# Even and odd columns of a matmul's moving operand in two halves of its tile

## The chip, the cores and the metric

The kernel runs on one core of one Trainium2 chip. The metric is the device time of one execution in microseconds (us); for the kernel before it is 2790.34 us, the median of three runs (2790.34 to 2790.83).

## The reference

One inference step of a decoder trunk with one layer, model width 2048, all in float32. 16 learned meta tokens and 256 prompt tokens form one sequence; 8 further tokens are single decode steps with recurrent states of their own. All 280 tokens share the weights:

```python
def swiglu(x, w_gate, w_up, w_down):
    return (jax.nn.silu(x @ w_gate) * (x @ w_up)) @ w_down
...
x = layer_norm(ALPHA * x + 0.5 * swiglu(x, f1_g, f1_u, f1_d), ln1_g, ln1_b)
m, s_ret, s_hg = token_mixer(x, pos, s_ret, s_hg, prompt, w_in, lb, hg_norm_g, w_out)
x = layer_norm(ALPHA * x + m, ln2_g, ln2_b)
x = layer_norm(ALPHA * x + 0.5 * swiglu(x, f2_g, f2_u, f2_d), ln3_g, ln3_b)
```

The FFN width is 5504. `token_mixer` projects x by one matrix to 10 x 2048 columns (q, k, v and gate of a retention branch with 8 heads, the same of an HGRN2 branch with 16 heads, and two merge gates), runs both recurrences in chunks, merges them and projects by `w_out`. The outputs are the tokens after the third norm (without the meta tokens) and the new states.

## The kernel before

Activations lie transposed: the 128 partitions hold 128 features, the columns are tokens. So x is 16 tiles of 128 x 280 (T = 280), and from the mixer's merge on 128 x 264 (TL = 264, without the meta tokens). Weights are the stationary operand in blocks of 128 x 128, and tokens are the moving operand.

For precision without plain-fp32 matmuls, each operand is split in two tiles of the rounded type fp32r: a high part (ScalarE casts, L198 for activations, L163 for weights) and a low part, the rest (VectorE subtracts, L199 and L164). `dense` (L179, its matmul is L193) then issues three products for each weight block: high x high, high weight x low activation, low weight x high activation. All add into one PSUM bank over the `nk` blocks of a sum.

The stages in order, each a stream of dense products on TensorE:

- FFN 1 up: 43 pairs of gate and up blocks, two pairs to a group of four banks, over 16 feature tiles, 280 columns (trace name `up`). The result goes through SiLU and a product into `sg` and is split into the hidden tiles `hh` and `hl` (43 of each).
- FFN 1 down: 16 output blocks over the 43 hidden tiles, 280 columns (`dn`).
- Mixer: the input projection in 8 units (head pairs); per unit first f, q_h, i_h, q_r, k_r, v_r, then the gates of the unit before (g_r, a_r, g_h, a_h), each two blocks of 128 features over 16 feature tiles (`pj_...`). The parts f, i_h, k_r, v_r have 280 columns, the other six 264: their moving operand starts at token 16. Two coroutines a unit (`mix_hg`, `mix_ret`) do the recurrences with small matmuls; `pump` moves each on after a number of product steps that its `yield` names.
- w_out: 16 blocks over 16 merge tiles `yh`, `yl`, 264 columns (`wo`).
- FFN 2 up and down, as FFN 1 with 264 columns.

The order of instructions on TensorE is written out by hand (it is the program's); a scheduler orders the other engines by priority. Weights are loaded by `stream` (L145) from SyncE's queue in units of 8 blocks, three buffers deep.

`x_tiles` (L231) hands out the moving tiles of x: each has 296 columns (XP), of which 280 or 264 are used from a start column that differs from tile to tile (0, 4, 8 or 12). `Norm` keeps a running residual `d`: `residual` (L262, operations L269 and L270) reads the high and low parts back, `shifted` (L302) may write a "lead" version of x before the mean is known (L318, L319: the rows by the norm's gain, one column of ones behind the tokens, one column of the bias behind that), and `normalise` (L357) writes the final x parts (L364, L365). `first` (L336) runs the first group of the next stage on the lead version.

## Time and profile before

| | |
|---|---|
| median of the runs | 2790.34 us |
| profiled execution's own span | 2787.6 us |
| TensorE busy, granted clock | 2777.1 us, 1.00 |
| TensorE weight loads busy | 2752.6 us |
| VectorE busy | 1735.2 us |
| ScalarE busy | 1362.0 us |
| DMA moved | 536.27 MB, mean 192 GB/s |

The profiled execution is not timed apart from its span: the span runs from the first to the last instruction, and the 2.7 us to the runs' median lie around it. In the profile PE is the matmul side of TensorE and PEld its weight loads, which overlap the matmuls; DVE is VectorE, ACT is ScalarE, POOL is GpSimd and SP is SyncE with the DMA queue. A matmul row's duration reaches from its start to its modelled end and overlaps the next one, so the step from one matmul to the next is shorter than the duration.

### The profile page before, as it was taken

Reading aid. Unit: us, or ns where it says so; the run is one execution under the profiler, and the core shown is the slowest. Engines: PE = TensorE matmul, PEld = TensorE weight load, DVE = VectorE, ACT = ScalarE, POOL = GpSimd, SP = SyncE. Lnnn points to the kernel's source line nnn. Section 1 sums busy time; section 2 is a strip of 40 time slices with the busy share of each in tenths; the row PEclk is TensorE's granted clock in tenths of the full one; section 3 lists DMA queues with packets and bytes.
Section 4 is the critical chain, followed back from the end, with each engine's and each line's share of the span. In section 5 each row is a group of like instructions: output and inputs, shape, how many; then the busy total and the mean of one; then the engine's idle time right before and its main releaser. Section 6 shows DMA issues by size and latency. Waiting matters only on the chain.

```text
span 2787.6 us, 54458 instructions
## 1 busy us (share of the span) xinstructions
PE 2777.1 (100%) x22576; PEld 2752.6 (99%) x22576; DVE 1735.2 (62%) x2937; ACT 1362.0 (49%) x2116; POOL 3.3 (0%) x38
## 2 busy tenths in 40 slices
PE   9999999999999999999999999999999999999999
PEld 9999999999999999999999999999999999999998
DVE  5444444464469777777777777776884444446544
ACT  5433343333356565656565656564554444444333
POOL 0000000000000000000000000000000000000000
PEclk9999999999999999999999999999999999999999
DMA  7555555555556676667666766665555555555554
GB/s 234 168 173 168 173 169 172 171 170 169 172 189 206 223 255 196 231 203 230 203 230 199 235 202 232 201 212 181 181 177 182 182 182 182 181 182 180 181 181 138
DMA packets 154584, 536.27 MB, mean 192 GB/s; under 512 B 17696, under 2 KB 25696, under 8 KB 154336
## 3 DMA queue, kind: packets, MB, share of 16 engines
q1 hardware_dynamic: 154048, 532.50, 59.4%
q8 instruction: 177, 2.90, 0.4%
q14 instruction: 71, 0.58, 0.1%
q10 hardware_dynamic: 288, 0.29, 0.0%
HBM read 502.12 MB, written 30.61 MB: 191 GB/s over the span
## 4 chain that ended last, share of the span: by engine, by line
PE 98%; DVE 1%; ACT 0%; issue 0%; DVEq 0%
PE up L193 37%; PE dn L193 19%; PE pj_f L193 4%; PE pj_v_r L193 4%; PE pj_i_h L193 4%; PE pj_g_r L193 3%; PE pj_q_h L193 3%; PE pj_g_h L193 3%; PE pj_q_r L193 3%; PE pj_a_h L193 3%; PE wo L193 3%; PE pj_a_r L193 3%; PE pj_k_r L193 3%; PE pqr L997 1%; PE psr L966 0%; PE psc L949 0%
## 5 line engine op out<-in xcount | busy, mean ns | idle before, releaser
L164 DVE TENSOR_TENSOR wlo<-raw,whi 128x1024 fp32r<-128x1024 f32 (+1 forms) x869 | 1062.5, 1223 | 866.4 <-ACT whi L163 863.3
L163 ACT CAST whi<-raw 128x1024 fp32r<-128x1024 f32 (+1 forms) x870 | 909.2, 1045 | 1104.2 <-PE up L193 478.5
L193 PE MATMUL up<-xl,whi 128*128 128x280 f32 (+1 forms) x2688 | 765.4, 288 | 0.0
L193 PE MATMUL up<-xh,wlo 128*128 128x280 f32 (+1 forms) x2688 | 765.1, 288 | 0.0
L193 PE MATMUL up<-xh,whi 128*128 128x280 f32 (+1 forms) x2688 | 764.3, 287 | 0.0
L193 PEld LDWEIGHTS up<-xh,wlo 128*128 128x128 f32 x2688 | 503.0, 188 | 0.2 <-DVE wlo L164 0.2
L193 PEld LDWEIGHTS up<-xh,whi 128*128 128x128 f32 x2688 | 503.0, 188 | 0.0
L193 PEld LDWEIGHTS up<-xl,whi 128*128 128x128 f32 x2688 | 502.7, 188 | 0.0
L193 PE MATMUL dn<-hh,whi 128*128 128x280 f32 (+1 forms) x1376 | 397.1, 289 | 0.0
L193 PE MATMUL dn<-hl,whi 128*128 128x280 f32 (+1 forms) x1376 | 395.8, 288 | 0.0
L193 PE MATMUL dn<-hh,wlo 128*128 128x280 f32 (+1 forms) x1376 | 395.7, 288 | 0.0
L193 PEld LDWEIGHTS dn<-hl,whi 128*128 128x128 f32 x1376 | 259.0, 188 | 0.1
L193 PEld LDWEIGHTS dn<-hh,whi 128*128 128x128 f32 x1376 | 258.9, 188 | 0.1
L193 PEld LDWEIGHTS dn<-hh,wlo 128*128 128x128 f32 x1376 | 258.7, 188 | 0.0
L193 PE MATMUL pj_g_r<-xh,whi 128*128 128x264 f32 x256 | 79.2, 309 | 0.0
L193 PE MATMUL pj_v_r<-xh,whi 128*128 128x280 f32 x256 | 75.9, 297 | 0.0
L193 PE MATMUL pj_g_h<-xh,whi 128*128 128x264 f32 x256 | 75.2, 294 | 0.0
L193 PE MATMUL pj_k_r<-xh,whi 128*128 128x280 f32 x256 | 75.0, 293 | 0.0
L193 PE MATMUL pj_i_h<-xh,whi 128*128 128x280 f32 x256 | 74.8, 292 | 0.0
L193 PE MATMUL pj_v_r<-xl,whi 128*128 128x280 f32 x256 | 74.6, 292 | 0.0
L193 PE MATMUL pj_i_h<-xl,whi 128*128 128x280 f32 x256 | 74.6, 291 | 0.0
L193 PE MATMUL pj_k_r<-xl,whi 128*128 128x280 f32 x256 | 74.6, 291 | 0.0
(379 smaller groups left out, 5219.4 us busy)
## 6 DMA issues: line engine op xcount, KB each, us to landing
raw<-in_w_up SPq DMA_DIRECT2D x343, 512.0 KB, 3.4
raw<-in_w_in SPq DMA_DIRECT2D x320, 512.0 KB, 3.7
raw<-in_w_dn SPq DMA_DIRECT2D x172, 512.0 KB, 3.4
smr<-in_sr SPq DMA_DIRECT2D x32, 512.0 KB, 4.8
out_srs<-smr SPq DMA_DIRECT2D x32, 512.0 KB, 6.3
raw<-in_w_out SPq DMA_DIRECT2D x32, 512.0 KB, 3.5
smh<-in_sg SPq DMA_DIRECT2D x16, 512.0 KB, 3.6
out_sgs<-smh SPq DMA_DIRECT2D x16, 512.0 KB, 6.2
```

The source lines that it names most:

```text
L163: nc.scalar.copy(hi[:, j:jn, :], raw[:, j:jn, :])
L164: nc.vector.tensor_tensor(out=lo[:, j0:j1, :], in0=raw[:, j0:j1, :], in1=hi[:, j0:j1, :].bitcast(F32), op=ALU.subtract)
L193: nc.tensor.matmul(o, w, t, start=start, stop=stop)
L997: nc.tensor.matmul(pq[32 * j : 32 * j + 32, 256 * e : 256 * e + 256], qdr[:, c, 32 * b : 32 * b + 32], sms[2 * e + c][:, j, :], start=c == ...
```

## The change

Every moving tile of a dense product (x, hidden and merge tiles, both parts) is kept in two halves: the first half holds the even columns, the second the odd ones. `Halves` presents such a tile as a pattern of (pair, even or odd), so that reading it in order gives column 0 from the first half, column 0 of the second half, then the next of each. `dense` reads the moving operand so and writes PSUM as pairs, in the usual column order. What writes these tiles (the splits, the lead, the final norm) and what reads them back (the residual) goes through the same pattern, while the other operand is read as pairs in order. The halves are 148 columns long in the x tiles, 140 or 132 in the hidden tiles and 132 in the merge tiles. The differing start columns of the x tiles are gone. The lead version sets two columns of ones and works on an even number of columns.

```diff
 
 WP = P + 4
 XP = 296
+XH = XP // 2
 
 WARM = 11
 
@@ -51,6 +52,23 @@
 SCORES = ((0, 0, SEQ, P), (SEQ, P - NMETA, 2 * P - P + NMETA, P), (2 * SEQ - P + NMETA, SEQ - NMETA, NMETA, LP - 2 * P))
 NSC = SCORES[2][0] + SCORES[2][2]
 GAMMA = [1.0 - 2.0 ** (-5.0 - h) for h in range(HR)]
+
+
+def pairs(x):
+
+    return x.rearrange("p (b a) -> p b a", a=2)
+
+
+class Halves:
+
+
+    def __init__(self, tile, half, n):
+        self.all = tile.rearrange("p (a b) -> p b a", b=half)
+        self.n = n
+
+    def __getitem__(self, cols):
+        c0, c1, _ = cols.indices(self.n)
+        return self.all[:, c0 // 2 : c1 // 2, :]
 
 
 def ffn_up_groups():
@@ -184,8 +202,8 @@
             todo = []
             for i in range(n):
                 wh, wl = block()
-                h, l = xhi[k][:, cols[i]], xlo[k][:, cols[i]]
-                o = outs[i][:, : h.shape[1]]
+                h, l = xhi[k][cols[i]], xlo[k][cols[i]]
+                o = pairs(outs[i][:, : 2 * h.shape[1]])
                 todo.append([(o, wh, h, k == 0, False), (o, wh, l, False, False), (o, wl, h, False, k == nk - 1)])
 
             for x in zip(*todo) if parts_in_turn else todo:
@@ -195,6 +213,8 @@
                 hook(k)
 
     def split(hi, lo, x):
+        if isinstance(hi, Halves):
+            hi, lo, x = hi[:], lo[:], pairs(x)
         nc.scalar.copy(hi, x)
         nc.vector.tensor_tensor(out=lo, in0=x, in1=hi.bitcast(F32), op=ALU.subtract)
 
@@ -229,9 +249,8 @@
     xl = [None] * KC
 
     def x_tiles(c, which, n=T):
-        for e, (x, nm) in enumerate(((xh, "xh"), (xl, "xl"))):
-            o = 4 * ((2 * c + e) // 8 % 2) + 8 * (c % 2) * e
-            x[c] = xp.tile([P, XP], F32R, tag=f"{nm}{c}", name=f"{nm}{which}_{c}")[:, o : o + n]
+        for x, nm in ((xh, "xh"), (xl, "xl")):
+            x[c] = Halves(xp.tile([P, XP], F32R, tag=f"{nm}{c}", name=f"{nm}{which}_{c}"), XH, n)
 
     def row_tile(name, n=T):
         return rp.tile([P, n], F32, tag=name, name=name)
@@ -263,13 +282,13 @@
 
             n = self.n
             a = ALPHA if self.whole else 2.0 * ALPHA
-            self.dx[m] = dx = row_tile(f"d{m}", T + 1)
+            self.dx[m] = dx = row_tile(f"d{m}", T + 2)
             self.d[m] = d = dx[:, :n]
-            x0 = xh[m].shape[1] - n
-            nc.vector.scalar_tensor_tensor(out=d, in0=xl[m][:, x0:].bitcast(F32), scalar=a, in1=other, op0=ALU.mult, op1=op)
-            nc.vector.scalar_tensor_tensor(out=d, in0=xh[m][:, x0:].bitcast(F32), scalar=a, in1=d, op0=ALU.mult, op1=ALU.add)
+            x0, o = xh[m].n - n, pairs(d)
+            nc.vector.scalar_tensor_tensor(out=o, in0=xl[m][x0:].bitcast(F32), scalar=a, in1=pairs(other), op0=ALU.mult, op1=op)
+            nc.vector.scalar_tensor_tensor(out=o, in0=xh[m][x0:].bitcast(F32), scalar=a, in1=o, op0=ALU.mult, op1=ALU.add)
             if self.lead:
-                nc.gpsimd.memset(dx[:, n : n + 1], 1.0)
+                nc.gpsimd.memset(dx[:, n : n + 2], 1.0)
 
         def chunk(self, m, f):
             if self.d[m] is not None:
@@ -314,12 +333,12 @@
             if self.lead:
                 x_tiles(m, f"g{self.which}", n + 2)
                 g = self.g[:, m : m + 1]
-                dx = self.dx[m][:, : n + 1]
-                nc.scalar.activation(xh[m][:, : n + 1], dx, AF.Identity, scale=g)
+                dx = pairs(self.dx[m][:, : n + 2])
+                nc.scalar.activation(xh[m][:], dx, AF.Identity, scale=g)
                 nc.vector.scalar_tensor_tensor(
-                    out=xl[m][:, : n + 1], in0=dx, scalar=g, in1=xh[m][:, : n + 1].bitcast(F32), op0=ALU.mult, op1=ALU.subtract)
-                nc.vector.tensor_copy(xh[m][:, n + 1 : n + 2], self.bs[:, 0, m : m + 1])
-                nc.vector.tensor_copy(xl[m][:, n + 1 : n + 2], self.bs[:, 1, m : m + 1])
+                    out=xl[m][:], in0=dx, scalar=g, in1=xh[m][:].bitcast(F32), op0=ALU.mult, op1=ALU.subtract)
+                nc.vector.tensor_copy(xh[m][n:][:, 0, 1:], self.bs[:, 0, m : m + 1])
+                nc.vector.tensor_copy(xl[m][n:][:, 0, 1:], self.bs[:, 1, m : m + 1])
 
         def stats(self):
             n = self.n
@@ -361,9 +380,9 @@
                 sub(d, d, self.mean)
                 nc.vector.scalar_tensor_tensor(out=d, in0=d, scalar=g, in1=self.r, op0=ALU.mult, op1=ALU.mult)
                 x_tiles(c, self.which, self.n)
-                nc.scalar.activation(xh[c], d, AF.Identity, bias=b)
+                nc.scalar.activation(xh[c][:], pairs(d), AF.Identity, bias=b)
                 nc.vector.scalar_tensor_tensor(
-                    out=xl[c], in0=d, scalar=b, in1=xh[c].bitcast(F32), op0=ALU.add, op1=ALU.subtract)
+                    out=xl[c][:], in0=pairs(d), scalar=b, in1=xh[c][:].bitcast(F32), op0=ALU.add, op1=ALU.subtract)
 
         def finish(self, out):
 
@@ -426,8 +445,8 @@
                     sg = hp.tile([P, n], F32, tag="sg", name=f"sg{m}", bufs=2)
                     nc.scalar.activation(sg, outs[j][:, :n], AF.Silu)
                     mul(sg, sg, outs[ng + j][:, :n])
-                    hh[m] = hp.tile([P, n], F32R, tag=f"hh{m}", name=f"hh{m}")
-                    hl[m] = hp.tile([P, n], F32R, tag=f"hl{m}", name=f"hl{m}")
+                    hh[m] = Halves(hp.tile([P, n], F32R, tag=f"hh{m}", name=f"hh{m}"), n // 2, n)
+                    hl[m] = Halves(hp.tile([P, n], F32R, tag=f"hl{m}", name=f"hl{m}"), n // 2, n)
                     split(hh[m], hl[m], sg)
             if before is not None:
 
@@ -490,7 +509,7 @@
         def parts(pool, cs):
             for n, x in (("yh", yh), ("yl", yl)):
                 for c in cs:
-                    x[c] = pool.tile([P, TL], F32R, tag=f"{n}{c}", name=f"{n}{c}")
+                    x[c] = Halves(pool.tile([P, TL], F32R, tag=f"{n}{c}", name=f"{n}{c}"), TL // 2, TL)
 
         yh, yl, ys = [None] * KC, [None] * KC, [None] * KC
         parts(yp, range(EARLY))
```

## Prediction, on record before the result

> **What bounds the kernel now.** I read the page first: busy times, the granted clock and the chain that ended last.

> ```profile
> span 2787.6 us, 54458 instructions
> ...
> PE 2777.1 (100%) x22576; PEld 2752.6 (99%) x22576; DVE 1735.2 (62%) x2937; ACT 1362.0 (49%) x2116; POOL 3.3 (0%) x38
> ...
> PEclk9999999999999999999999999999999999999999
> ...
> PE 98%; DVE 1%; ACT 0%; issue 0%; DVEq 0%
> ```

> TensorE is busy for 2777.1 of 2787.6 us, 98% of the last chain is its own, and the granted clock is full in all forty slices. So nothing that the other engines do is worth more than a few microseconds, and the time is a number of products times what one product takes. The chain in order of time tells what one takes (start, length, what, how many):

> ```profile
> 5.57 532.05 PE up L193 x4128
> ...
> 557.39 246.59 PE dn L193 x1914
> ...
> 1950.98 67.56 PE wo L193 x555
> ...
> 2027.90 491.27 PE up L193 x4056
> 2537.92 233.51 PE dn L193 x1914
> ```

> In FFN 1 the moving tiles have 280 columns, and a product takes 532.05/4128 = 128.9 ns and 246.59/1914 = 128.8 ns. With 264 columns it is 67.56/555 = 121.7, 491.27/4056 = 121.1 and 233.51/1914 = 122.0 ns. These are the two numbers that the change can move.

> The next question is whether they are as low as the engine goes. The groups by shape, and one tile's own row (lowest/median/highest ns), answer that. A row's duration is longer than the step from one product to the next, since products overlap (291 ns for a step of 128.9), but differences between widths are differences of the step:

> ```profile
> L193 PE MATMUL up<-xh,whi 128*128 128x280 f32 x1376 | 393.1, 291 | 0.0
> ...
> L193 PE MATMUL up<-xh,whi 128*128 128x264 f32 x1312 | 371.2, 283 | 0.0
> ...
> L966 PE MATMUL psr<-vs,ks 128*128 128x256 f32 x112 | 15.8, 281 | 0.0
> ...
> L729 PE MATMUL pl<-Qm,K 128*128 128x192 f32 x64 | 11.7, 326 | 0.0
> ...
> L1011 PE MATMUL por<-dtab,vtr 128*128 128x256 f32 x32 | 9.5, 379 | 0.0
> ...
> L1011 PE MATMUL por<-dtab,vtr 128*128 128x144 f32 x32 | 6.5, 286 | 0.0
> ```

> ```profile
> L204 PE MATMUL pd<-prodsmh,ones_r x8: 393/396/399, 865.1 to 1785.3; 128*128 128x512 f32 x8
> ```

> Lines 193, 966 and 204 multiply the rounded type fp32r in one pass; lines 1011 and 729 multiply plain fp32, which the trace records as two passes. One fp32 pass costs (379 - 286)/112 = 0.830 ns a column. One fp32r product costs (396 - 281)/256 = 0.449 ns a column. Twice the speed of an fp32 pass would be 0.415, so the fp32r stream runs 0.034 ns a column (8%) behind. This loss grows with the columns (the rows of 256 and 512 give it), so it is not one fixed price for each new weight block; it belongs to the moving stream, the thing that the change re-lays. The fp32 row at 192 columns, whose moving operand is three separate runs of 64, lies on the fp32 line: 286 + 48 x 0.830 = 326. So a second dimension in the moving pattern, and two jumps in it, cost nothing at the fp32 pace.

> **The change part by part.** It adds and removes no matmul, no weight load, no DMA and no wait. It changes the address of each column: consecutive columns come from places 592 bytes apart (x tiles, half of 296 columns), 560 or 528 bytes apart (hidden tiles, half of 280 or 264) or 528 (merge tiles), and back by that minus 4. PSUM is still written in order.

> *Products.* Of the loops, 280 columns go through 43 x 2 x 16 x 3 = 4128 products of FFN 1 up, 16 x 43 x 3 = 2064 of FFN 1 down, and 64 x 16 x 3 = 3072 of the input projection (f, i_h, k_r, v_r): 9264. At 264 columns there are 4128 and 2064 of FFN 2, 96 x 16 x 3 = 4608 of the projection and 16 x 16 x 3 = 768 of w_out: 11568. (The first groups of two stages have two columns more, which I leave out.) No row shows a moving tile read at alternating places, so the price has two ends. If two open places let the stream run at its full pace, a product of 280 loses 280 x 0.034 = 9.5 ns and one of 264 loses 9.0: 9264 x 9.5 + 11568 x 9.0 = 88 + 104 = 192 us less. If each column has to be fetched by itself and the stream falls to the pace of an fp32 pass, it is 0.830 - 0.449 = 0.381 ns a column more, 106.7 and 100.6 ns a product: 988 + 1164 = 2152 us more. The nearest rows do not decide: the three-run row tells of two jumps in 192 columns at half the pace, here there is a jump at every column at full pace. I take the gain, because a loss that grows with the columns at full pace and is nil at half pace looks like one place of the store that cannot answer fast enough, and two places used in turn each have to answer at only half the rate.

> [...]

> *What is late next if products shorten.* Weight loading comes close. A group of short products with full weight blocks shows its pace:

> ```profile
> 886.90 0.84 PE pl L757 x8
> ```

> That is 105 ns for a product of 64 columns, whose columns alone take 64 x 0.830 = 53 ns, so I read 105 as the load of 128 weights. Shortened products would take 128.9 - 9.5 = 119.4 and 121.4 - 9.0 = 112.4 ns, still above it. The other engines come next (start and end of the stretch, its length, then busy times of PE, PEld, DVE, ACT and POOL with counts, clock, DMA share, GB/s):

> ```profile
> 804.00:866.00 62.00, 61.98 (x483) 61.46 (x482) 58.34 (x123) 43.16 (x75) 0.99 (x2) 1.00 0.60 193
> 866.00:900.00 34.00, 32.72 (x264) 31.95 (x264) 33.05 (x85) 21.47 (x54) 0.00 (x0) 1.00 0.68 226
> ...
> 1180.00:1864.00 684.00, 684.00 (x5741) 671.21 (x5739) 508.69 (x1039) 395.06 (x735) 0.79 (x8) 1.00 0.66 217
> ```

> From 804 to 900 us VectorE is busy 91.4 of 96 us, so that stretch cannot shorten: its 747 products give back 747 x 9.3 ns = 7 us of the gain. In the steady mixer one head pair takes 139.28 us (two starts of the same piece):

> ```profile
> 1319.91 4.63 PE pj_f L193 x36
> ...
> 1459.19 4.63 PE pj_f L193 x36
> ```

> It holds 8 x 48 products of 280 and 12 x 48 of 264, which would save 384 x 9.5 + 576 x 9.0 = 8.8 us, 6%. VectorE's share there goes from 74% to 79%. The mixer's threads wait for a fixed number of product steps, and those steps get shorter while the vector chains do not, so I count a third of it as lost over some 7.5 such periods: 22 us.

> *Writers and readers of the halves.* The splits (L198, L199), the normalise pair (L364, L365), the lead pair (L318, L319) and the two residual operations (L269, L270) keep their counts and sizes (one column more in the lead), but write or read with the jump. Rows:

> ```profile
> L198 ACT CAST hh<-sg x86: 406/418/427, 35.9 to 2520.1; 128x280 fp32r<-128x280 f32 x43, 128x264 fp32r<-128x264 f32 x43
> ```

> ```profile
> L199 DVE TENSOR_TENSOR hl<-sg,hh 128x280 fp32r<-128x280 f32 x43 | 17.3, 444 | 0.0
> ...
> L199 DVE TENSOR_TENSOR prodvbh<-pr,prodsmh 128x256 fp32r<-128x256 f32 x40 | 15.5, 418 | 0.0
> ...
> L207 DVE TENSOR_TENSOR pr<-Q,K 128x256 f32<-128x256 f32 x24 | 9.4, 420 | 0.2
> ...
> L365 DVE SCALAR_TENSOR_TENSOR xl<-d,lnp,xh 128x280 fp32r<-128x280 f32 x16 | 7.4, 499 | 0.0
> ...
> L901 DVE TENSOR_TENSOR vtr<-vtr,cen 128x512 f32<-128x512 f32 x8 | 5.5, 690 | 0.2
> ```

> The lower end is nil: the 24 products "pr" read every second or fourth column and take 420 ns where unbroken operands take 418. The upper end is twice the time a column, (690 - 444)/232 = 1.06 ns, or 0.30 us an operation. I take nil for ScalarE and most of VectorE, whose extra 0.6 us per hidden pair would lie beside some 24.7 us of products (192 x 128.9 ns) in which both engines are about half idle. Only at 804 to 900 us is the cover gone: 16 operations of line 365 at up to 0.30 us, 5 us, which I count. The last hidden tile is used after 41 x 3 products of the down pass (15.9 us), so stage ends stay covered. The wider memset on POOL is not on the chain.

> Sum: 192 - 7 - 22 - 5 = 158 us; I take 150, since the whole of the 0.034 going is the upper end. The median of the runs is 2790.34 us, 2.7 above the profiled span, with only the time around the span between; 2790.3 - 150 = 2640 us.

> **Rivals.** First, on the other side: half pace. The moving port keeps one place open, each column opens a new one, and products take 129 + 107 = 236 and 121.4 + 100.6 = 222 ns. Everything else is then hidden under TensorE, the mixer included: 2790 + 2152 = 4942 us. It decides from the point where a jump costs more than the 0.034 ns a column now lost. [...] Against: the store serves more than one stream at once already, since each product's weights load under the one before. [...] Second, a part of that: only some jumps are slow. With one column in four at the fp32 pace the loss is a quarter, 538 us, and the time 3328 us. Third, the loss is not in the place that is read (a clock crossing, say): products keep 129 and 121 ns, and only VectorE's 5 us at 804 to 900 us may show: 2790 to 2795 us.

> **How the numbers follow.** Gain 0.48; half pace 0.36; a part of it 0.10; no effect 0.06, of which 0.05 within 0.2% (5.6 us, about what a measurement of this kernel can tell from no change) and 0.01 above. So faster 0.48, same 0.05, slower 0.47. The likeliest single case is the gain, with a range of its own of 2598 (all 192 us) to 2740 us (a third of the 150 us). As both signs hold most of the chance, the range has to reach over the half pace: 2595 to 4960 us.

> **What would show it.** Right: the long pieces of the chain at some 120 ns a product in FFN 1 and 113 in FFN 2, the row of 280 columns near 282 ns, DVE's share above 64%, new waits of PE on DVE in the mixer and around 850 us. Half pace: 236 and 222 ns, the row near 398 ns, VectorE's share at 35%. No effect: the rows as they are. The splits' rows (418, 444 ns) tell whether a jump costs the other engines anything. The prediction is wrong in its main step if the products get longer.

## The result

The changed kernel takes 2630.63 us (median of four runs, 2628.61 to 2631.78) against 2790.34 us before: a ratio of 0.9428, 95% interval 0.9414 to 0.9441. That is 160 us less; the prediction was 2640 us. The profiled execution took 2630.44 us with a span of 2628.7 us.

The page of the changed kernel, its busy times, clock, and chain by engine:

```profile
span 2628.7 us, 54448 instructions
...
PE 2602.0 (99%) x22576; PEld 2569.1 (98%) x22576; DVE 1758.9 (67%) x2937; ACT 1388.5 (53%) x2116; POOL 3.3 (0%) x38
...
PE 83%; DVE 9%; DMA 4%; ACT 2%; issue 1%; SPq 0%; DVEq 0%; ACTq 0%
```

TensorE has the same 22576 matmuls in 175 us less, and is no longer the whole chain: VectorE has 9% of it and transfers 4%, where both had next to nothing. The chain in order of time (start, length, what, how many) has the long stages:

```profile
10.66 488.37 PE up L211 x4096
499.04 17.88 PE dn L211 x150
517.38 228.10 PE dn L211 x1914
...
2397.14 215.32 PE dn L211 x1914
```

A product of 280 columns now takes 488.37/4096 = 119.2 and 228.10/1914 = 119.2 ns (128.9 before), one of 264 columns 215.32/1914 = 112.5 ns (122.0). The groups by shape of the changed kernel:

```profile
L211 PE MATMUL up<-xh,whi 128*128 128x280 f32 x1376 | 381.4, 283 | 0.2 <-ACT whi L181 0.2
...
L211 PE MATMUL up<-xh,wlo 128*128 128x264 f32 x1312 | 362.3, 276 | 0.2 <-DVE wlo L182 0.2
...
L985 PE MATMUL psr<-vs,ks 128*128 128x256 f32 x112 | 16.1, 284 | 0.2 <-DVE ks L957 0.2
```

The small products `psr`, which the change leaves in one piece, have not got shorter (281 before, 284 now), so it is the layout and not the clock. What got longer are the operations that write the halves, on VectorE (by shape) and ScalarE (the tile's row):

```profile
L219 DVE TENSOR_TENSOR hl<-sg,hh 128x280 fp32r<-128x280 f32 x43 | 24.8, 655 | 0.2 <-ACT hh L218 0.2
...
L384 DVE SCALAR_TENSOR_TENSOR xl<-d,lnp,xh 128x280 fp32r<-128x280 f32 x16 | 10.0, 711 | 0.1
...
L289 DVE SCALAR_TENSOR_TENSOR d<-xh,d 128x280 f32<-128x280 f32 x16 | 6.7, 450 | 0.1
```

```profile
L218 ACT CAST hh<-sg x86: 674/698/732, 34.9 to 2380.7; 128x280 fp32r<-128x280 f32 x43, 128x264 fp32r<-128x264 f32 x43
```

Writing in turn costs 0.2 to 0.3 us an operation (444 to 655, 499 to 711, 418 to 698 ns). Reading in turn costs next to nothing: line 289, which reads x back, takes 450 ns where it took 440 before:

```profile
L270 DVE SCALAR_TENSOR_TENSOR d<-xh,d 128x280 f32<-128x280 f32 x16 | 7.0, 440 | 0.0
```

By stage, from the starts of the first products of each stage in the two traces (us; head pairs are the mixer's units):

| stage | before | after | change | dense products |
|---|---|---|---|---|
| FFN 1 up | 532.1 | 493.1 | -39.0 | 4128 of 280 |
| FFN 1 down | 266.4 | 246.4 | -19.9 | 2064 of 280 |
| mixer, head pair 1 | 79.5 | 82.3 | +2.8 | 576 |
| mixer, head pair 2 | 154.4 | 156.6 | +2.1 | 960 |
| mixer, the other six | 886.1 | 836.1 | -50.1 | 6144 |
| w_out | 94.5 | 89.7 | -4.8 | 768 of 264 |
| FFN 2 up | 500.6 | 469.7 | -30.9 | 4128 of 264 |
| FFN 2 down | 252.1 | 232.5 | -19.6 | 2064 of 264 |

At 9.7 ns a product of 280 and 9.0 of 264 the six later pairs could give 2304 x 9.7 + 3840 x 9.0 = 57 us and gave 50. The first two could give 14 and took 5 more. Those, 7 us of the later pairs, some 6 of FFN 2 up's 37 and 2 of w_out's 7 are where the gain did not arrive.

### The profile page after: what moved, and what is told of

It is laid out like the page before. It is cut to its first block, busy times and chain, and to the rows that moved or that the text cites. A ratio compares the mean times of both kernels' runs of the same rounds, so it can differ in the third digit from the quotient of the medians.

```text
span 2628.7 us, 54448 instructions
## 1 busy us (share of the span) xinstructions
PE 2602.0 (99%) x22576; PEld 2569.1 (98%) x22576; DVE 1758.9 (67%) x2937; ACT 1388.5 (53%) x2116; POOL 3.3 (0%) x38
## 4 chain that ended last, share of the span: by engine, by line
PE 83%; DVE 9%; DMA 4%; ACT 2%; issue 1%; SPq 0%; DVEq 0%; ACTq 0%
PE up L211 35%; PE dn L211 18%; DVE wlo L182 3%; PE pj_q_h L211 3%; PE pj_v_r L211 3%; PE pj_f L211 3%; PE pj_k_r L211 3%; PE pj_i_h L211 3%; PE pj_q_r L211 2%; PE pj_g_r L211 2%; PE pj_g_h L211 2%; PE pj_a_h L211 2%; PE pj_a_r L211 2%; PE wo L211 2%; DMA smr<-in_sr 1%
## 5 line engine op out<-in xcount | busy, mean ns | idle before, releaser
L211 PE MATMUL up<-xl,whi 128*128 128x280 f32 (+1 forms) x2688 | 743.4, 279 | 2.3 <-DVE xl L384 2.3
L211 PE MATMUL up<-xh,whi 128*128 128x280 f32 (+1 forms) x2688 | 743.6, 280 | 0.9 <-DVE rt L370 0.6
L211 PE MATMUL up<-xh,wlo 128*128 128x280 f32 (+1 forms) x2688 | 743.4, 279 | 0.2 <-DVE wlo L182 0.2
L211 PE MATMUL dn<-hh,whi 128*128 128x280 f32 (+1 forms) x1376 | 384.7, 280 | 0.0
L211 PE MATMUL dn<-hl,whi 128*128 128x280 f32 (+1 forms) x1376 | 384.3, 279 | 0.0
L211 PE MATMUL dn<-hh,wlo 128*128 128x280 f32 (+1 forms) x1376 | 384.3, 279 | 0.0
L211 PE MATMUL pj_i_h<-xh,wlo 128*128 128x280 f32 x256 | 72.9, 285 | 1.2 <-DVE wlo L182 1.2
L211 PE MATMUL pj_k_r<-xh,whi 128*128 128x280 f32 x256 | 73.1, 286 | 0.0
L211 PE MATMUL pj_v_r<-xh,wlo 128*128 128x280 f32 x256 | 72.8, 284 | 0.1
```

Source lines behind the costliest of these rows:

```text
L211: nc.tensor.matmul(o, w, t, start=start, stop=stop)
```

## The experiments

The theory at the start (1), a guess: the moving port cannot be fed at full pace from one place of the store, but can from two in turn. Its rivals, guesses too: the two places have to differ in an address bit (2), the pattern in two dimensions is what counts (3), or the start columns that the change also removes.

**The other part of the change alone.** The kernel before, without the differing start columns:

```diff
-            o = 4 * ((2 * c + e) // 8 % 2) + 8 * (c % 2) * e
+            o = 0
```

> The kernel before, with all x tiles starting at column 0 of their buffers (the other part of the change alone: the differing start columns go, the halves do not come). Theory 1: the loss is in reading one place at full pace, wherever it starts, so the products keep 121 and 129 ns and the ratio to before is 0.998 to 1.004. Rival: the start columns were what kept the loss at 8%, or caused it; then the up and projection rows move by several ns (over 1% of the time) while dn stays.

Measured: 2791.75 us, ratio 1.0005 (0.9996 to 1.0015). The start columns brought nothing in plain order and their removal costs nothing. The whole gain is the halves'.

**Distances.** The hidden tiles of the changed kernel in seven layouts at once, told apart by a letter in the tile's name, so that the products of one run show each layout's price (this probe and its two successors, on orders and on streams, ran once each and took 2635.8, 3007.89 and 2648.95 us, with their slow layouts in them; only the rows within a run are compared):

```diff
-                    hh[m] = Halves(hp.tile([P, n], F32R, tag=f"hh{m}", name=f"hh{m}"), n // 2, n)
+                    L, kind, arg = layout_of(m, n)
+                    hh[m] = Lay(hp, kind, arg, n, f"hh{m}", f"hh{L}{m}")
```

> The changed kernel, with the 43 hidden tiles of both FFNs laid out in seven ways (A to G, a letter in the tile's name); everything else as changed. A: one piece in order, as before. The others: two halves whose starts lie apart by B 560 or 528 bytes (as changed), C 576, D 568, E 640, F 1024, G 564 bytes. Theory 1 (the moving port cannot be fed at full pace from one place, but can from two in turn, wherever they are): rows of dn at 280 and 264 columns near 291 and 284 ns for A, near 283 and 276 ns for B to G. Theory 2 (the two places must lie in different halves of the store by one address bit, and the changed distances are odd multiples of 16 bytes): B at 283 and 276, but C, E and F, even multiples of 16, at 291 and 284 or slower; D and G between. Theory 3 (it is the pattern in two dimensions, not the places): no difference by distance either, so this run does not tell it from theory 1.

The groups by shape of that run, A (one piece), then distances of 560, 576 and 1024 bytes:

```profile
L254 PE MATMUL dn<-hhA,wlo 128*128 128x280 f32 x128 | 37.2, 291 | 0.0
...
L254 PE MATMUL dn<-hhB,wlo 128*128 128x280 f32 x128 | 36.2, 283 | 0.0
...
L254 PE MATMUL dn<-hhC,wlo 128*128 128x280 f32 x128 | 36.2, 283 | 0.0
...
L254 PE MATMUL dn<-hhF,wlo 128*128 128x280 f32 x32 | 9.0, 283 | 0.0
```

Theory 2 falls: all six distances give 283 ns, D, E and G too. Side by side in one stage, A keeps the loss.

**Orders.** The same probe with other orders of places.

> The changed kernel, with the 43 hidden tiles of both FFNs in seven orders of places; everything else as changed. B: two halves, a column from each in turn (as changed). Q: four parts in turn, 304 bytes apart. E: eight parts in turn, 144 bytes apart. P: two halves, two neighbouring columns from each in turn. T: one piece, first every second column, then the others (step 8 bytes). S: one piece with a step of 16 bytes. W: a step of 112 bytes (280 columns) or 48 bytes (264). Theory 1 (full pace needs more than one place in turn): B, Q, E and P near 283 and 276 ns at 280 and 264 columns; T, which stays in one place, near 291 and 284 as the tiles in one piece; S and W, which reach a new place at each column, near 283 and 276. Theory 3 (the pattern in two dimensions is enough): T near 283 and 276 too. [...]

```profile
L256 PE MATMUL dn<-hhS,wlo 128*128 128x280 f32 x96 | 42.2, 439 | 0.0
...
L256 PE MATMUL dn<-hhT,wlo 128*128 128x280 f32 x96 | 41.8, 436 | 0.0
...
L256 PE MATMUL dn<-hhE,wlo 128*128 128x280 f32 x96 | 40.8, 425 | 0.0
...
L256 PE MATMUL dn<-hhP,wlo 128*128 128x280 f32 x96 | 34.1, 355 | 0.0
...
L256 PE MATMUL dn<-hhB,wlo 128*128 128x280 f32 x112 | 31.6, 283 | 0.0
...
L256 PE MATMUL dn<-hhQ,wlo 128*128 128x280 f32 x96 | 30.6, 318 | 0.0
```

None of these theories stands. T, a step of only 8 bytes in one piece, was to cost what one piece costs (1) or nothing (3) and took 436 ns. S should have been quick (1) and took 439, W 445. More places in turn are worse (Q 318, E 425), and so are two columns from each half (P 355). In the timeline three products with layout T start 250 ns apart:

```profile
700.68 0.43 PE L256 MATMUL dn<-hhT,whi 128*128 128x280 f32 x1
700.93 0.43 PE L256 MATMUL dn<-hlT,whi 128*128 128x280 f32 x1
701.18 0.44 PE L256 MATMUL dn<-hhT,wlo 128*128 128x280 f32 x1
```

**Streams.** The probe with layouts that separate them; the view of J and N is

```diff
+            self.all = t.rearrange("p (g a b) -> p g b a", a=2, b=arg // 2)
```

with groups of 4 (J) and 8 (N) columns.

> The changed kernel, with the hidden tiles in five layouts. A: one piece. B: two halves (as changed). J: one piece in groups of four columns, even, even, odd, odd. N: one piece in groups of eight, four even, then four odd. H: two halves as B, but in each half a column takes only every second place (step 8 bytes). Theory 5 (the even columns and the odd columns of the moving operand are fetched by two streams, each in lines of 16 bytes, and a stream can open a line each 1.8 ns and no faster): a line that yields two columns of a stream lasts only 1.67 ns and costs 8%, one that yields four costs nothing, one that yields one costs 1.8 ns a pair of columns. So A and J near 291 and 284 ns (280 and 264 columns), B and N near 283 and 276 although N lies in one piece, and H, with two columns a line, near 290 and 283 although it lies in two halves. Theory 1 (two places far apart are what helps): J and N as A, H near 283 and 276. Theory 5b (two streams, but the loss is that both want the same line at once): N and H near 283 and 276, J near 291 and 284.

```profile
L264 PE MATMUL dn<-hhN,wlo 128*128 128x280 f32 x176 | 49.7, 283 | 0.0
...
L264 PE MATMUL dn<-hhA,wlo 128*128 128x280 f32 x160 | 46.6, 291 | 0.0
...
L264 PE MATMUL dn<-hhJ,wlo 128*128 128x280 f32 x160 | 46.6, 291 | 0.0
...
L264 PE MATMUL dn<-hhB,wlo 128*128 128x280 f32 x160 | 45.2, 283 | 0.0
...
L264 PE MATMUL dn<-hhH,wlo 128*128 128x280 f32 x32 | 9.2, 286 | 0.0
```

N, in one piece with four even columns and then four odd, takes 283 ns like the halves, and J, two and two, 291 like plain order: theory 1 is refuted, and even and odd columns count apart, as two streams would have it. H, in two halves but with two columns a line, takes 286 to 287 ns, between the two ends; its products start 125 ns apart in the median, 125/70 = 1.79 ns a line as in T:

```profile
739.18 0.29 PE L264 MATMUL dn<-hhH,whi 128*128 128x280 f32 x1
739.31 0.28 PE L264 MATMUL dn<-hlH,whi 128*128 128x280 f32 x1
739.43 0.29 PE L264 MATMUL dn<-hhH,wlo 128*128 128x280 f32 x1
```

So, by the same estimate, of the loss in one piece some 6 of 9.7 ns (119 to 125) go with the rate of opening lines, and the last 3 to 4 (125 to 129) come where both streams use the same lines (A and J share them, H does not). That sharing costs these 3 to 4 ns is argued from these rows and not shown: T's streams share their lines too and S's do not, and T is not the slower (250 and 254 ns). Theories 5 and 5b each hold part of it.

Three layouts stay unexplained by a plain rate: Q takes 318 ns where a new line for each column of a stream would give the 436 of T; P's products start 180 ns apart, between the 125 of two columns a line and the 250 of one; and W, with a step of 48 bytes at 264 columns, takes 514 ns (a start each 0.32 us, at full clock too), more than the 419 of S with a line for each column. Whether a stream holds more than one line, and what else 48 bytes hit, was not tried.

P's row in the run with other orders is about 408 ns at 264 columns, more than at 280 (355 to 357). That is the clock and not the layout. In FFN 2 down of that run the granted clock falls to 0.50 for 3.4 to 6.8 us in each of the 16 output blocks, in W's products or just behind them, without a wait of TensorE in that stage, and P follows W. Where it comes back, P's starts go from 220 ns apart to 170, the same 0.64 ns a column as 180 at 280 columns:

```profile
2579.31 0.42 PE L256 MATMUL dn<-hhP,whi 128*128 128x264 f32 x1
2579.53 0.42 PE L256 MATMUL dn<-hlP,whi 128*128 128x264 f32 x1
...
2580.51 0.34 PE L256 MATMUL dn<-hhP,whi 128*128 128x264 f32 x1
2580.68 0.34 PE L256 MATMUL dn<-hlP,whi 128*128 128x264 f32 x1
```

The stretches around it (length, busy PE, PEld, DVE, ACT, POOL, clock, DMA share, GB/s):

```profile
2576.00:2580.00 4.00, 4.00 (x17) 3.73 (x16) 0.00 (x0) 0.01 (x1) 0.00 (x0) 0.58 0.42 131
2580.00:2600.00 20.00, 20.00 (x107) 18.28 (x107) 12.59 (x25) 6.35 (x8) 0.00 (x0) 1.00 0.33 106
```

**Writing the halves in order.** From the splits in the run with other orders one sees what writing costs: VectorE's low parts in layouts that put two successive columns within 16 bytes (T 448 ns, P 442) cost no more than one piece did in the kernel before (444), those with one (B 653, S 694) 0.2 us more:

```profile
L264 DVE TENSOR_TENSOR hlB<-sg,hhB 128x280 fp32r<-128x280 f32 x7 | 4.1, 653 | 0.2 <-ACT hhB L263 0.2
...
L264 DVE TENSOR_TENSOR hlS<-sg,hhS 128x280 fp32r<-128x280 f32 x6 | 4.0, 694 | 0.0
...
L264 DVE TENSOR_TENSOR hlT<-sg,hhT 128x280 fp32r<-128x280 f32 x6 | 2.5, 448 | 0.0
...
L264 DVE TENSOR_TENSOR hlP<-sg,hhP 128x280 fp32r<-128x280 f32 x6 | 2.5, 442 | 0.0
```

The version that avoids this walks half by half on both sides:

```diff
-            hi, lo, x = hi[:], lo[:], pairs(x)
+            hi, lo, x = hi.major(), lo.major(), halves(x)
...
-                nc.scalar.activation(xh[c][:], pairs(d), AF.Identity, bias=b)
+                nc.scalar.activation(xh[c].major(), halves(d), AF.Identity, bias=b)
...
```

> The changed kernel, but the splits, the lead and the final norm walk through the columns half by half: they write each half in order and read their sources with a step of two columns. Products as changed. In the changed kernel the operations that write the halves in turn got longer (final norm low part 499 to 711 ns, split 444 to 669 ns). Theory 1: it is writing in turn that costs VectorE and ScalarE, reading with a step of 8 bytes is free (the product pr reads so in 420 ns), so these rows go back to about 499 and 444 ns, and where VectorE bounds (the first 90 us of the mixer, the start of FFN 2) some 5 to 10 us are won: about 2622 us, ratio to before 0.937 to 0.941. Rival: stepped reading costs as much, the rows stay near 700 ns and the ratio at 0.943.

```profile
L226 DVE TENSOR_TENSOR hl<-sg,hh 128x280 fp32r<-128x280 f32 x43 | 17.3, 443 | 0.0
...
L391 DVE SCALAR_TENSOR_TENSOR xl<-d,lnp,xh 128x280 fp32r<-128x280 f32 x16 | 7.4, 500 | 0.0
```

VectorE's rows are back at 443 and 500 ns (ScalarE's cast of `hh` at 451, from 698), and the time is 2622.61 us, ratio 0.9405 (0.939 to 0.9421). As that interval still touches the changed kernel's, both ran again on one chip, in five rounds.

> The changed kernel itself, for a comparison on the same chip with the version that writes the halves in order: ratio to before 0.9415 to 0.944.

> The version that writes the halves in order, beside the changed kernel on one chip. If the gain seen (2622.6 against 2630.6 us) is one of VectorE's time where VectorE bounds, it is there again: some 5 to 10 us below the changed kernel, ratio to before 0.939 to 0.942. Rival: the difference was one of chips, and both are the same within 2 us.

The changed kernel took 2632.71 us, ratio 0.9438 (0.9425 to 0.945), and the version that writes in order 2625.4 us, ratio 0.9406 (0.9393 to 0.9418): 7 us less, again, with intervals apart. In the two profiles, 3.4 us of that lie in the first two head pairs, 1.8 in FFN 2 up and 1.2 in w_out. This version is faster than both kernels.

**Where the rest of the gain went.** Two kernels that leave work out, run once each, ask what sets the pace in the first two head pairs.

```diff
+                        if u < 2:
+                            continue
                         nc.vector.scalar_tensor_tensor(
                             out=sm[:, b, :], in0=vb[:, b, :], scalar=fk
...
```

> The changed kernel without VectorE's multiply-add that updates the decode states in the first two of the eight mixer units (their decode states and sample outputs then lack the new token): 64 operations of some 0.48 us and 0.35 us less, about 26 us of VectorE's time, no transfer less. It asks where 32 of the 192 us went that the shorter products could give; the first two units take 239 us in the changed kernel and 234 us before, though their 1536 dense products need 14 us less. Theory A: VectorE sets the pace there, and TensorE, made to wait over 3 us at a time, then runs at half clock for a while (granted clock 0.50 from 929 to 933 us). Then the stretch takes 220 to 228 us and the whole 2617 to 2625 us, with fewer stretches of clock under 1. Rival B: the decode states' transfers set the pace (they appear in the chain); then the stretch keeps 236 us or more.

Measured: 2625.56 us, and the two pairs take 82.9 + 149.8 = 232.7 us. Between the two theories, and told apart by pair: the first does not change at all (82.9 against 82.3), the second gains 6.8 us. So the states' arithmetic is part of what holds the second. In the first no gain shows; its time at half clock, 6.8 us against 3.4 (see below), can hide up to 1.7 us.

```diff
+            kept = 0 < u < keep
+            lo = state["lo"] if kept else wp.tile([P, U, WP], F32R, tag="wlo", name=f"wlo{u}")[:, :, :P]
...
+                    if kept:
+                        continue
...
+            block = stream(A["w_in"], keep=24)
```

> The changed kernel, but in the first 24 weight units of the mixer's projection (those of its first head pair) only the first unit's low part is computed and is used for all 24 (the low products of that pair then use wrong weights): 23 subtractions of 1.22 us less on VectorE, 28 us, all in the first 82 us of the mixer, with as many products and transfers. The run without the state updates left that stretch as it was (82.9 against 82.3 us; 79.5 before). Theory A, narrowed: there VectorE is full (29.9 of 30 us) with the final norm, the weights' low parts and the first head pair's chains, and it sets the pace. Then the stretch falls to between 70 and 76 us (its 576 dense products and the small ones need about 70), and the whole to 2619 to 2625 us. Rival B: transfers or the hand-written waits set the pace; the stretch keeps 80 us or more.

The first pair falls from 82.3 to 73.1 us, the second from 156.6 to 152.5, and the whole to 2617.38 us, a little below the range that was expected. The stretch's rows, first of the changed kernel and then of this one (length, busy PE, PEld, DVE, ACT, POOL, clock, DMA share, GB/s):

```profile
775.00:805.00 30.00, 26.65 (x217) 25.25 (x216) 29.92 (x59) 19.40 (x33) 0.00 (x0) 1.00 0.51 160
```

```profile
776.00:806.00 30.00, 29.48 (x248) 28.92 (x247) 22.17 (x67) 21.13 (x37) 0.00 (x0) 1.00 0.60 195
```

With VectorE relieved, from 29.9 to 22.2 of 30 us, TensorE does 248 matmuls in the stretch and not 217. So in the first pair VectorE sets the pace; up to 1.7 of the 9.2 us can be the half clock, of which this run has none there.

There is also the clock. In the second pair TensorE waits once for VectorE's scaled keys. This wait was 1.5 us before and is 3.5 us in the changed kernel, where a wait of 2.0 us for `K` follows (the lists of waits, before and after: us in total, times, longest):

```profile
PE psc L949 <- DVE ks L938: 1.5, 1, 1.5
```

```profile
PE psc L968 <- DVE ks L957: 3.5, 1, 3.5
...
PE ptk L845 <- DVE K L227: 2.0, 1, 2.0
```

The stretches around the longer wait are:

```profile
925.00:929.00 4.00, 0.52 (x3) 0.31 (x2) 3.87 (x11) 3.92 (x12) 0.00 (x0) 0.87 0.70 241
929.00:933.00 4.00, 4.00 (x17) 3.33 (x17) 3.36 (x14) 2.58 (x10) 0.00 (x0) 0.50 0.72 262
933.00:941.00 8.00, 8.00 (x65) 8.00 (x64) 5.70 (x16) 5.64 (x13) 0.00 (x0) 0.89 0.27 75
```

At the end of the 3.5 us without work the granted clock falls to 0.50 and stays there for 6.8 us (by the shares 1.0 us of the first stretch, the whole second and 1.8 us of the third). TensorE works for some 6 of them, 17 matmuls in 4 us, so by estimate this wait costs about twice its length. 3.4 us at half clock also stand behind the wait of 2.0 us and, in the first pair, behind two waits of 1.0 and 1.3 us close together:

```profile
962.00:965.00 3.00, 3.00 (x21) 2.35 (x23) 2.20 (x5) 1.67 (x6) 0.00 (x0) 0.52 0.93 321
```

```profile
812.00:815.00 3.00, 3.00 (x15) 3.00 (x14) 2.28 (x6) 1.49 (x3) 0.00 (x0) 0.50 0.86 339
```

In the kernel before, waits of 1.3 and 1.5 us in the same pairs brought no half clock. How short a wait has to be was not settled.

What is settled: the first pair is bound by VectorE, the second in part by VectorE's state updates; without them the wait for `K` and the half clock behind it are gone as well, while the wait for the scaled keys stays (3.3 us). The 10.2 us at half clock in the second pair can be at most 5 of the 11 us of gain that are missing there. What share falls to the states' transfers that also stand in its chain was not separated.

## Why the prediction was right

- *The terms of the step.* The gap of 0.034 ns a column between the measured 0.449 and half an fp32 pass (0.415) was read as a loss that can go. It went whole: 9.5 ns predicted and 9.7 measured at 280 columns, 9.0 and 9.0 (121.5 to 112.5) at 264. The pace is now (119.2 - 112.5)/16 = 0.42 ns a column.
- *The reason given for it.* Only half right. That the loss belongs to the moving stream and its layout was confirmed, and an answer of the store that is too slow at full pace fits the estimate of 1.8 ns a line. That two places are needed was not confirmed: layout N gets the same in one piece, and Q and E show that more places in turn lose. By the estimate, what counts in the layouts that a plain rate explains is how many columns each of two streams takes from a line, and the change raises that from two to four. That two halves are one of the orders that do this was luck as far as the reason goes.
- *The rival at half pace.* It did not come for this layout, though it exists: T and S, where by the estimate a stream gets one column from a line, cost 250 and 254 ns where 236 was named. Its chance of 0.36 was the author's estimate: no row of before told what a jump at each column costs. The runs have the whole scale, by the estimated columns of a stream in a line: 119 ns with four (the change), 125 with two (H), 250 with one (T).
- *The stretch that VectorE fills.* 7 us were counted as lost at 804 to 900 us, and 5 as the price of writing there. Head pair 1 gave nothing of its 5 us and took 2.8 more: the step was right, and the run with the kept low parts shows its cause.
- *The mixer's waits.* 22 us were counted, spread evenly. The sum over the mixer is near (19 us lost in the first two pairs, 7 later), but the place was wrong, so that it came out near is luck: pairs three to seven gave 8.2, 7.9, 8.7, 8.2 and 6.4 of their 8.8 us. Their share of VectorE did not matter. Pair 2 lost 11, partly to a half clock that no step of the prediction had.
- *Writing in turn.* Nil was taken and the upper end, 0.30 us an operation, is nearly what came: 0.21 to 0.28. Its cover held, as said, in the FFN's splits; it was not counted at the start of FFN 2. Of the 6 us lost there, writing in order gives back only 1.8, so most of that loss is something else; TensorE waits there 2.3 us for the low parts of the final norm (`xl`). In all, writing in order gets 7 us back.
- *The sum.* 192 - 34 = 158 us was worked out and 150 taken. The span shortened by 158.9 us; the caution of 8 us was the error. That the losses add up to about the 34 us counted is partly luck, since FFN 2 up and w_out, which were not counted, lost 8 of them.

## What to carry to other kernels

Where a matmul's step grows with its columns faster than half an fp32 pass of the same trace does (here 0.449 against 0.415 ns a column), the moving operand's layout is to be suspected: in fp32r, four even columns and then four odd (or two halves) ran 8% faster here than plain order (119 against 129 ns). Write such a layout in its own order, half by half, and read the source with the step: with two successive elements within 16 bytes VectorE's writes took 442 to 448 ns here, as in plain order (444), and with one such element 653 to 694. When TensorE gets faster, look for the first stretches where another engine is full, and read the granted clock behind each new wait: here it was 0.50 for 6.8 us behind one of 3.5 us, and for 3.4 us behind one of 2.0 us.

## What the runs showed of the hardware that was not expected

- A moving fp32r operand of 280 columns took 119 ns when even and odd columns lie in two halves or, four and four in turn, in one piece, 129 in plain order, 250 with a step of 8 bytes (first all even columns of the plain order), and 254 with one of 16 bytes: the small step is as bad as the larger one.
- Two interleaved pieces gave the same rows of 283 ns at each of six distances from 560 to 1024 bytes at 280 columns, some of them no multiple of 16; products started each 150 ns with four pieces, each 243 with eight and each 119 with the halves.
- VectorE and ScalarE wrote alternately to two halves at about 0.8 to 1.0 ns a column more, but VectorE read from them at hardly any extra cost (440 and 450 ns).
- The granted clock fell to 0.50 without any wait of TensorE: in FFN 2 down of the run with other orders, in the products of layout W (a step of 48 bytes, 0.32 us each) or just behind them, in each of the 16 output blocks.
